# A hybrid attention and RWKV-7 encoder layer: gate products bound to the scan's products, two PSUM banks for the solved values, and PSUM tiles of its own for the first stage

## The chip, the cores and the metric

The kernel runs on one core of a Trainium2 chip, as one launch. The metric is the device time of that launch in microseconds (us); lower is better. TensorE (PE) multiplies, VectorE (DVE), ScalarE (ACT) and GpSimd (POOL) do the elementwise work, and SyncE (SP) issues the transfers between DRAM and the on-chip memory. Products land in PSUM, which has eight banks of 512 float32 columns.

## The reference

One layer over 1040 positions (16 learned ones and 1024 of the input) with 1024 channels. A normalised input is projected to everything that the two mixing branches need; the branches are merged through sigmoid gates; a gated MLP follows.

```python
proj = hn @ w_in
q, k, v, f_logit, rw, gates = jnp.split(proj, IN_SPLITS, axis=-1)
...
o_fox = fox_attention(qh, kh, vh, fcum)
...
def rwkv7_scan(r, w, k, v, a, bb):
    '''S_t = S_{t-1} diag(w_t) + (S_{t-1} a_t) bb_t^T + v_t k_t^T ;  y_t = S_t r_t.'''
...
yn = (y - mean) * lax.rsqrt(var + GN_EPS)
...
g_fox, g_rwkv = jnp.split(jax.nn.sigmoid(gates + g_b), 2, axis=-1)
merged = g_fox * (o_fox @ w_bf) + g_rwkv * (o_rwkv @ w_br)
```

The scan is the serial part: the state of one position enters the next. The gates depend on the normalised input alone.

## The kernel before

Channels lie on the 128 partitions and positions along the free dimension, in three chunks of some 340 to 386 columns. Float32 products are made as three products of rounded halves (`mm3`: high by high, low by high, high by low), so one tile of 1024 input channels takes 24 product instructions, three for each of eight slices of the channels. A scheduler orders each engine's instructions from the order in which the program emits them; each engine then works strictly in that order.

**Stage 0** (`stage0`) loads the input, takes root mean squares (`stats`, with `rsqrt_rows`, whose inverse root is a bit trick and Newton iterations on a few columns), writes the normalised input as high and low parts (`norm`), and makes three low-rank projections for each chunk (`lora`): twelve products a chunk (line 173), each copied out by ACT into a tile `o` (three buffers) and stored to DRAM by SP. Its products use the PSUM pool that later serves attention (tags `S` and `M`), and the low-rank products share the banks `A` and `B` (use `pr`) with the next stage.

**Stages 1 and 2** are three streams that are emitted side by side: `att` (attention), `rec` (first `prep`, the projections and factors of the scan, use `pr`; then the scan), and `gat` (the gates). The scan is cut into 17 chunks of 64 positions. A chunk (`rw_chain`) is a chain: eight products from the state (line 523, the right sides), a copy by ACT (525), eight products with the inverted triangle (534, the solved values), copies by ACT and DVE (535, 536), eight products for the next state (541), an addition by DVE (544); beside it 16 products give the chunk's output (549, 551), which goes to DRAM. Each chunk's operands come by nine transfers (`rw_load`, lines 497 to 506), one chunk ahead. The inversion itself (`solve`) is done for six chunks at a time. After chunks 5, 10 and 16 `group_norm` normalises the finished positions, with two products (873, 878) for each of four channel tiles.

**The gates** are 16 tiles by three chunks of 24 products each, 1152 in all, each chunk copied out by ACT (856) and stored. They are emitted once the scan's pool exists, 13 tiles at first and the last three once the scan has been emitted. Where they stand between the scan's products was up to the scheduler.

Stage 3 multiplies the branches by their output weights, stage 4 is the output projection with the second norm, stage 5 the MLP.

Of the kernel before, what the change touches and what calls it, by code (L numbers as in the profile page):

```python
# [102 lines left out]
def stage0(S):  # L103
# [8 lines left out]
    with tc.tile_pool(name="s0", bufs=1) as p0:  # L112
# [47 lines left out]
        def lora(c):  # L160
            t0, t1 = G[c]
            n = t1 - t0
            sg, wa = T("sg", 1), T("wa", 1)
            rw_tile(S, 0, sg[:, :n], w0[0], c)
            nc.scalar.activation(out=sg[:, :n], in_=sg[:, :n], func=AF.Tanh, scale=0.5)
            nc.gpsimd.tensor_scalar(out=sg[:, :n], in0=sg[:, :n], scalar1=0.5, scalar2=0.5, op0=ALU.mult, op1=ALU.add)
            rw_tile(S, 1, wa[:, :n], w0[1], c)
            nc.scalar.activation(out=wa[0:64, :n], in_=wa[0:64, :n], func=AF.Tanh)
            for p in range(NP_):
                pc = slice(p * P, (p + 1) * P)  # L170
                for i, (l, r) in enumerate(((lup[0:64, pc], wa[0:64, :n]), (lup[64:128, pc], wa[64:128, :n]), (gup[:, pc], sg[:, :n]))):
                    ps = psum(S, "pr")
                    nc.tensor.matmul(ps[:, :n], lhsT=l, rhs=r, start=True, stop=True)
                    o = T("o", 3)
                    if i == 2:
                        nc.scalar.copy(out=o[:, :n], in_=ps[:, :n])
                    else:
                        S.tanh = nc.scalar.activation(out=o[:, :n], in_=ps[:, :n], func=AF.Tanh, scale=0.5, bias=(S.w0h, S.a0h)[i][:, p:p + 1])
                    if i == 0:
                        nc.gpsimd.tensor_scalar(out=o[:, :n], in0=o[:, :n], scalar1=0.5, scalar2=0.5, op0=ALU.mult, op1=ALU.add)  # L180
                    nc.sync.dma_start(out=(S.sw_d, S.tha_d, S.g_d)[i][p, :, t0:t1], in_=o[:, :n])
# [57 lines left out]
def psum(S, tag):  # L239

    slots = S.psb[tag]
    n = S.psn[tag] % len(slots)
    S.psn[tag] += 1
    t = slots[n]
    if n and slots[n - 1] == t:
        return S.half[tag][:, 512:1024]
    S.half[tag] = slot(S, t, tag)
    return S.half[tag][:, 0:512]
# [261 lines left out]
def rw_chain(S, c):  # L510
    nc, rp = S.nc, S.rp
    if c == 0:
        S.ld_c = rw_load(S, 0)
    uv, w1, am, ar, bkt = S.ld_c
    if c < NCH - 1:
        S.ld_c = rw_load(S, c + 1)
    z, zn = S.zb[c % 2], S.zb[(c + 1) % 2]
    at = S.at[c // 6][:, 4 * (c % 6):4 * (c % 6) + 4]
    H = [(h, h // 2, h % 2, slice(64 * (h % 2), 64 * (h % 2) + 64)) for h in range(8)]
    quads = lambda ps: ps[:, :256].rearrange("p (q v) -> p q v", v=64)  # L520
    pv = quads(psum(S, "ch"))
    for h, q, e, r in H:
        nc.tensor.matmul(pv[r, q, :], lhsT=w1[:, h, :], rhs=z[e][:, q, :], start=True, stop=True)  # L523
    pt = rp.tile([P, 4, 64], F32, name="pt", bufs=1)
    nc.scalar.copy(out=pt[:], in_=pv)
    zw = rp.tile([P, 4, 64], F32, name="zw", bufs=1)
    if c < NCH - 1:
        for e in range(2):
            r = slice(64 * e, 64 * e + 64)
            nc.gpsimd.tensor_tensor(out=zw[r], in0=z[e][r], in1=S.wc[r, c, :].unsqueeze(2).broadcast_to([64, 4, 64]), op=ALU.mult)  # L530
    yield 1.0
    pu = quads(psum(S, "ch"))
    for h, q, e, r in H:
        nc.tensor.matmul(pu[r, q, :], lhsT=at[r, q, :], rhs=pt[r, q, :], start=True, stop=True)  # L534
    nc.scalar.copy(out=uv[0][0:64], in_=pu[0:64])
    nc.vector.tensor_copy(out=uv[1][64:128], in_=pu[64:128])
    yield 1.0
    if c < NCH - 1:
        pz = quads(psum(S, "ch"))
        for h, q, e, r in H:  # L540
            nc.tensor.matmul(pz[r, q, :], lhsT=bkt[:, q, r], rhs=uv[e][:, q, :], start=True, stop=True)  # L541
        for e in range(2):
            r = slice(64 * e, 64 * e + 64)
            nc.vector.tensor_tensor(out=zn[e][r], in0=pz[r], in1=zw[r], op=ALU.add)
        yield 1.0
    py = quads(psum(S, "ch"))
    for q in range(4):
        for h, _, e, r in H[2 * q:2 * q + 2]:
            nc.tensor.matmul(py[r, q, :], lhsT=z[e][:, q, :], rhs=ar[e][:, q, :], start=True, stop=False)  # L549
        for h, _, e, r in H[2 * q:2 * q + 2]:  # L550
            nc.tensor.matmul(py[r, q, :], lhsT=uv[e][:, q, :], rhs=am[:, h, :], start=False, stop=True)  # L551
    yt = rp.tile([P, 4, 64], F32, name="yt", bufs=1)
    nc.scalar.copy(out=yt[:], in_=py)
    n = min(64, L - 64 * c)
    nc.sync.dma_start(out=S.y_d[:, :, 64 * c:64 * c + n].rearrange("q p t -> p q t"), in_=yt[:, :, :n])
    yield 1.0
# [56 lines left out]
def rsqrt_rows(S, pool, ps, sq, n, ind, w, eps):  # L613
# [14 lines left out]
    nc.vector.tensor_scalar(out=v, in0=ps[:m, o:o + W], scalar1=eps, scalar2=None, op0=ALU.add)  # L628

    nc.vector.tensor_scalar(out=y.bitcast(I32), in0=v.bitcast(I32), scalar1=-0.5, scalar2=1597463007.0, op0=ALU.mult, op1=ALU.add)  # L630
    for _ in range(4):
        nc.vector.tensor_tensor(out=t, in0=v, in1=y, op=ALU.mult)
        nc.vector.scalar_tensor_tensor(out=t, in0=t, scalar=-0.5, in1=y, op0=ALU.mult, op1=ALU.mult)
        nc.vector.scalar_tensor_tensor(out=y, in0=t, scalar=1.5, in1=y, op0=ALU.add, op1=ALU.mult)
# [209 lines left out]
            now = t  # L844


def gates(S, ms):

    nc = S.nc
    for m in ms:  # L850
        w = wload(S, S.A["w_gate"][m], KD)
        for t0, t1 in CW:
            ps = psum(S, "gate")
            mm3(S, ps[:, :342], w, xwin(S, t0 + 2, 342))
            sg = S.cp.tile([P, 342], F32, name="sg", bufs=2)
            nc.scalar.activation(out=sg[:], in_=ps[:, :342], func=AF.Identity, bias=S.par("gate_b", m))  # L856
            nc.sync.dma_start(out=S.sg_d[m, :, t0 - T0:t1 - T0], in_=sg[:])
            yield 3.8


def group_norm(S, c):
# [29 lines left out]
def stage12(S):  # L891

    nc, tc = S.nc, S.tc
    banks(S, mm="S S M M", st="t o", pr="A B", t="t", o="o")
    pq_cm = tc.tile_pool(name="ps1", bufs=1, space=PSUM)
    S.pq = pq_cm.__enter__()
    p1_cm = tc.tile_pool(name="p1", bufs=1, side="right")
    p1 = p1_cm.__enter__()
    S.smask = p1.tile([P, 384], BF16, name="smask")
    nc.gpsimd.memset(S.smask[:], 1.0)  # L900
    nc.gpsimd.memset(S.smask[:].rearrange("p (c t) -> p c t", t=64)[:, :, 0:1], 0.0)
    stage0(S)
    banks(S, mm="S M")
    S.op = S.rp = None
    S.scanned = False
    S.ev = 0

    def att():
# [16 lines left out]
    def rec():  # L925
# [29 lines left out]

        S.of_cm = tc.tile_pool(name="of", bufs=1, side="right")
        S.ofp = S.of_cm.__enter__()
        S.scanned = True
        yield from merge_streams([(0.0, 1.0, group_norm(S, 2)), (0.0, 1.0, fox_load(S))])

    def gat():
        while S.rp is None:
            yield 1.0
        yield from gates(S, range(13))

        while not S.scanned:
            yield 1.0
        yield from gates(S, range(13, 16))

    for _ in merge_streams([(0.0, 1.0, att()), (0.0, 1.2, rec()), (0.0, 1.0, gat())]):  # L970
        pass
# [353 lines left out]
```

## Time and profile before

| | |
|---|---|
| median of 3 runs | 1916.93 us (1916.77 to 1916.99) |
| the profiled execution, its own time | 1909.92 us |
| its span, first to last instruction | 1908.1 us |
| PE busy | 1809.4 us, 95% |
| DVE, ACT, POOL busy | 57%, 40%, 39% |
| first low-rank product of the first chunk to last of the third | 41.05 to 108.7 us |
| first product of the scan | 738.26 us |
| last product of the scan | some 966.5 us |

The span is cut into stretches, and in each PE's busy time is multiplied by the clock that was granted to it (as a share of full speed): what is missing from the stretch's length is the time in which PE did not work at full pace.

### The profile page before, as it was taken

To read this page: it belongs to the slowest core of one execution; us is meant where nothing else is said; L and a number is where in the kernel's file an instruction comes from. 1 tells how busy PE (TensorE), PEld (TensorE's weight loads), DVE (VectorE), ACT (ScalarE), POOL (GpSimd) and SP (SyncE) were. 2 spreads that over 40 slices of the span, in tenths; PEclk is the share of its full clock that TensorE was granted. 3 is DMA by queue.
4 is the path that set the end of the run, shared out by engine and by line. 5 is a ranking of instruction groups with operands and counts; after the bars stand their busy time and mean duration, and the time that the engine had idled before them with its cause. 6 is when DMAs were issued, how large, how long until landed. Compare 5 with 4: busy or idle time off the path is not lost.

```text
span 1908.1 us, 33665 instructions
## 1 busy us (share of the span) xinstructions
PE 1809.4 (95%) x12756; PEld 1629.3 (85%) x12756; DVE 1086.0 (57%) x2024; ACT 764.4 (40%) x1684; POOL 748.4 (39%) x817
## 2 busy tenths in 40 slices
PE   5899999899999899999978999999999999999999
PEld 4589779679788588989868998998998999989997
DVE  6224644655746766632445538668567575585655
ACT  5345534443635532233455324433332332333331
POOL 4134224222414322233323235347346365474464
PEclk9899999799999899999998999999999999999999
DMA  5221331241423364675663334111112111111113
GB/s 179 102 66 46 81 82 54 68 105 53 99 65 82 77 150 123 169 192 162 190 177 113 116 117 126 45 45 47 48 39 67 45 38 63 51 40 56 45 45 116
DMA packets 197577, 170.83 MB, mean 90 GB/s; under 512 B 93768, under 2 KB 154744, under 8 KB 197416
## 3 DMA queue, kind: packets, MB, share of 16 engines
q1 hardware_dynamic: 197160, 168.62, 30.9%
q8 instruction: 101, 1.65, 0.4%
q14 instruction: 60, 0.49, 0.1%
q0 software_dynamic: 256, 0.07, 0.0%
HBM read 122.57 MB, written 46.06 MB: 88 GB/s over the span
## 4 chain that ended last, share of the span: by engine, by line
PE 57%; DVE 2%; DMA 2%; ACT 1%; POOL 1%; issue 1%; SPq 1%; ACTq 0%; DVEq 0%; POOLq 0%
PE mm L218 11%; PE mm L219 11%; PE mm L220 11%; PE dn L220 4%; PE dn L218 4%; PE dn L219 4%; PE gate L218 3%; PE gate L219 3%; PE gate L220 3%; DMA y<-y_d 1%; PE ch L541 1%; PE ch L534 0%; PE ch L523 0%; PE ch L551 0%; PE ch L549 0%
## 5 line engine op out<-in xcount | busy, mean ns | idle before, releaser
L206 POOL TENSOR_TENSOR wl<-wf,wh 128x512 fp32r<-128x512 f32 (+1 forms) x228 | 295.9, 1301 | 532.7 <-ACT wh L205 520.1
L219 PE MATMUL mm<-x,wh 128*128 128x344 f32 (+1 forms) x1056 | 338.5, 321 | 0.0
L220 PE MATMUL mm<-x,wl 128*128 128x344 f32 (+1 forms) x1056 | 336.9, 320 | 0.9 <-POOL wl L206 0.9
L218 PE MATMUL mm<-x,wh 128*128 128x344 f32 (+1 forms) x1056 | 336.6, 320 | 0.0
L205 ACT CAST wh<-wf 128x512 fp32r<-128x512 f32 (+1 forms) x228 | 138.7, 610 | 175.7 <-PE mm L219 70.4
L220 PEld LDWEIGHTS mm<-x,wl 128*128 128x128 f32 x1056 | 198.9, 189 | 1.7 <-POOL wl L206 1.5
L219 PEld LDWEIGHTS mm<-x,wh 128*128 128x128 f32 x1056 | 199.2, 189 | 0.4
L218 PEld LDWEIGHTS mm<-x,wh 128*128 128x128 f32 x1056 | 199.0, 189 | 0.5
L1171 DVE TENSOR_TENSOR h<-h,dn 128x512 f32<-128x512 f32 x240 | 153.1, 683 | 34.9 <-PE dn L220 28.6
L218 PE MATMUL gate<-xh,wh 128*128 128x342 f32 x384 | 127.4, 332 | 4.6 <-ACT sg L856 2.3
L219 PE MATMUL gate<-xl,wh 128*128 128x342 f32 x384 | 127.2, 331 | 0.0
L220 PE MATMUL gate<-xh,wl 128*128 128x342 f32 x384 | 126.6, 330 | 0.0
L218 PE MATMUL mm<-xh,wh 128*128 128x348 f32 (+5 forms) x336 | 116.9, 348 | 4.1 <-DVE sg L269 1.9
L219 PE MATMUL mm<-xl,wh 128*128 128x348 f32 (+5 forms) x336 | 113.9, 339 | 1.8 <-POOL xl L158 1.2
L220 PE MATMUL mm<-xh,wl 128*128 128x348 f32 (+5 forms) x336 | 112.5, 335 | 0.0
L218 PE MATMUL dn<-gx,wh 128*128 128x512 f32 x280 | 110.3, 394 | 0.0
L219 PE MATMUL dn<-gx,wh 128*128 128x512 f32 x280 | 110.2, 393 | 0.0
L220 PE MATMUL dn<-gx,wl 128*128 128x512 f32 x280 | 109.8, 394 | 0.0
L1138 DVE SCALAR_TENSOR_TENSOR uv<-mm,par,uv 128x342 f32<-128x342 f32 (+1 forms) x66 | 37.7, 571 | 108.9 <-ACT uv L1137 108.9
L218 PE MATMUL pr<-xh,wh 128*128 128x386 f32 (+1 forms) x288 | 95.9, 333 | 1.4 <-ACT bt L469 1.4
L220 PE MATMUL pr<-xh,wl 128*128 128x386 f32 (+1 forms) x288 | 94.8, 329 | 0.0
L219 PE MATMUL pr<-xl,wh 128*128 128x386 f32 (+1 forms) x288 | 94.8, 329 | 0.0
(326 smaller groups left out, 4325.2 us busy)
## 6 DMA issues: line engine op xcount, KB each, us to landing
wf<-in_w_up_dram SPq DMA_DIRECT2D x88, 256.0 KB, 2.7
wf<-in_w_down_dram SPq DMA_DIRECT2D x40, 256.0 KB, 2.7
sg_d<-sg SPq DMA_DIRECT2D x48, 171.0 KB, 3.3
sg<-sg_d SPq DMA_DIRECT2D x48, 171.0 KB, 2.3
wf<-in_w_gate_dram SPq DMA_DIRECT2D x32, 256.0 KB, 4.7
wf<-in_w_out_dram SPq DMA_DIRECT2D x32, 256.0 KB, 2.8
wf<-in_w_rw_dram SPq DMA_DIRECT2D x28, 256.0 KB, 2.7
wf<-in_w_qkv_dram SPq DMA_DIRECT2D x24, 256.0 KB, 2.9
```

The source lines that it names most:

```text
L205: nc.scalar.copy(out=wh[:, :n], in_=wf[:, :n])
L206: nc.gpsimd.tensor_tensor(out=wl[:, :n], in0=wf[:, :n], in1=wh[:, :n], op=ALU.subtract)
L218: nc.tensor.matmul(ps, lhsT=wh, rhs=xh, start=first and k == 0, stop=False)
L219: nc.tensor.matmul(ps, lhsT=wh, rhs=xl, start=False, stop=False)
L220: nc.tensor.matmul(ps, lhsT=wl, rhs=xh, start=False, stop=last and k == n - 1)
L541: nc.tensor.matmul(pz[r, q, :], lhsT=bkt[:, q, r], rhs=uv[e][:, q, :], start=True, stop=True)
L1138: nc.vector.scalar_tensor_tensor(out=t[:, :n], in0=ps[:, 1:1 + n], scalar=cw(1), in1=t[:, :n], op0=ALU.mult, op1=ALU.add)
L1171: nc.vector.tensor_tensor(out=half(r, c), in0=half(r, c), in1=ps[:], op=ALU.add if sign > 0 else ALU.subtract)
```

## The change

- **Gates.** One slice of the channels (three products, an eighth of a tile's chunk) is now emitted at a time, and each is ordered behind the latest of the scan's product groups (`S.hop`: the last product of lines 523, 535 and 542 of the new kernel). An eighth counts 0.53 in the streams' pacing while the scan runs and 0.33 before; a scan chunk counts 4.8, so nine eighths go with a chunk. All 16 tiles are one run; the wait for the scan's end is gone.
- **Two banks.** The solved values of the even and of the odd heads go to a PSUM bank each, so ACT and DVE copy from different banks.
- **The first stage** has a PSUM pool of its own: four single banks, two for its projections (`mm`) and two for the low-rank products (`lr`). The banks `A` and `B` are left to `prep`. The pool of attention is opened when stage 0's is closed. `o` has five buffers instead of three.
- `rsqrt_rows` makes three Newton iterations instead of four.

```diff
-                    ps = psum(S, "pr")
+                    ps = psum(S, "lr")
                     nc.tensor.matmul(ps[:, :n], lhsT=l, rhs=r, start=True, stop=True)
-                    o = T("o", 3)
+                    o = T("o", 5)
...
-    pu = quads(psum(S, "ch"))
+
+    pu = [quads(psum(S, "ch")) for _ in range(2)]
     for h, q, e, r in H:
-        nc.tensor.matmul(pu[r, q, :], lhsT=at[r, q, :], rhs=pt[r, q, :], start=True, stop=True)
-    nc.scalar.copy(out=uv[0][0:64], in_=pu[0:64])
-    nc.vector.tensor_copy(out=uv[1][64:128], in_=pu[64:128])
+        S.hop = nc.tensor.matmul(pu[e][r, q, :], lhsT=at[r, q, :], rhs=pt[r, q, :], start=True, stop=True)
+    nc.scalar.copy(out=uv[0][0:64], in_=pu[0][0:64])
+    nc.vector.tensor_copy(out=uv[1][64:128], in_=pu[1][64:128])
...
-    for _ in range(4):
+    for _ in range(3):
...
-def gates(S, ms):
+def gates(S):
...
-    for m in ms:
+    for m in range(16):
         w = wload(S, S.A["w_gate"][m], KD)
         for t0, t1 in CW:
             ps = psum(S, "gate")
-            mm3(S, ps[:, :342], w, xwin(S, t0 + 2, 342))
+            x = xwin(S, t0 + 2, 342)
+            for k in range(KD):
+                with S.tc.issue_after(S.hop.ins) if S.hop is not None else nullcontext():
+                    mm3(S, ps[:, :342], w[k:k + 1], x[k:k + 1], first=k == 0, last=k == KD - 1)
+                yield 0.53 if S.hop is not None else 0.33
...
-    banks(S, mm="S S M M", st="t o", pr="A B", t="t", o="o")
-    pq_cm = tc.tile_pool(name="ps1", bufs=1, space=PSUM)
-    S.pq = pq_cm.__enter__()
+
+    banks(S, mm="0 1", st="t o", lr="2 3", pr="A B")
...
-    stage0(S)
-    banks(S, mm="S M")
+    with tc.tile_pool(name="ps0", bufs=1, space=PSUM) as S.pq:
+        stage0(S)
+    pq_cm = tc.tile_pool(name="ps1", bufs=1, space=PSUM)
+    S.pq = pq_cm.__enter__()
+    banks(S, mm="S M", t="t", o="o")
```

How the instructions stand, at three places. First PE's queue in stage 0, at the low-rank products (line 173; `wa` and `sg` are their right sides, `lup` and `gup` the weights) of the second chunk. Before, they follow one another:

```order
L173 MATMUL pr<-wa,lup 128x384
L173 MATMUL pr<-sg,gup 128x384
L173 MATMUL pr<-wa,lup 128x384 x2
L173 MATMUL pr<-sg,gup 128x384
L173 MATMUL pr<-wa,lup 128x384 x2
L173 MATMUL pr<-sg,gup 128x384
L173 MATMUL pr<-wa,lup 128x384 x2
L173 MATMUL pr<-sg,gup 128x384
```

And now, at the same products:

```order
L173 MATMUL lr<-wa,lup 128x384
L219 MATMUL pr<-xl,wh 128x274
L220 MATMUL pr<-xh,wl 128x274
L173 MATMUL lr<-sg,gup 128x384
L218 MATMUL pr<-xh,wh 128x274
L219 MATMUL pr<-xl,wh 128x274
L220 MATMUL pr<-xh,wl 128x274
...
L173 MATMUL lr<-wa,lup 128x384 x2
L218 MATMUL pr<-xh,wh 128x386
L219 MATMUL pr<-xl,wh 128x386
L173 MATMUL lr<-sg,gup 128x384
```

The scan's input projections (`pr`) have moved in between. In all 96 of them (72 of 386 columns, 24 of 274) now stand ahead of stage 0's last low-rank product, where none did; 32 products of the forget gate's logits (line 580 of before), which stood ahead of it, now stand behind it. At the third group of attention's transposes (line 689 of before) both queues have the same products behind them.

Second, PE's queue in the scan's first chunk, between the right sides (523) and the solved values (534 before, 535 now); `wh` and `wl` are a gate tile's weights. Before, 22 gate products stand there, of which these are the last:

```order
L220 MATMUL gate_8080<-xh_97,wl_7830 128x342
L218 MATMUL gate_8080<-xh_98,wh_7829 128x342
L219 MATMUL gate_8080<-xl_106,wh_7829 128x342
L220 MATMUL gate_8080<-xh_98,wl_7830 128x342
L218 MATMUL gate_8080<-xh_99,wh_7829 128x342
L219 MATMUL gate_8080<-xl_107,wh_7829 128x342
L220 MATMUL gate_8080<-xh_99,wl_7830 128x342
L534 MATMUL ch_7998<-pt_7952,at_7028 64x64 x8
```

And now, all that stands there:

```order
L218 MATMUL gate_8037<-xh_94,wh_7823 128x342
L219 MATMUL gate_8037<-xl_102,wh_7823 128x342
L220 MATMUL gate_8037<-xh_94,wl_7824 128x342
L218 MATMUL gate_8037<-xh_95,wh_7823 128x342
L219 MATMUL gate_8037<-xl_103,wh_7823 128x342
L220 MATMUL gate_8037<-xh_95,wl_7824 128x342
L535 MATMUL ch_8103<-pt_8078,at_7026 64x64 x4
```

A chunk held 57 to 59 gate products before (22, 22, 1 to 3, and 12), until they ran out at its fifteenth chunk; now it holds 27 (6, 6 to 9, 6 to 9, 6). Ahead of the scan's first product stand 263 gate products before and 339 now.

Third, PE's queue behind the scan's last output product. Before, the gates are used up, and the branch products of stage 3 (`orw`, `ofx`) stand between the last statistics products (`gn`):

```order
L220 MATMUL mm<-orw,wl 128x342
L873 MATMUL gn<-y,bo_197 128x342
L218 MATMUL mm<-ofx,wh 128x342
L219 MATMUL mm<-ofx,wh 128x342
L220 MATMUL mm<-ofx,wl 128x342
```

And now:

```order
L219 MATMUL gate<-xl,wh 128x342
L220 MATMUL gate<-xh,wl 128x342
L218 MATMUL gate<-xh,wh 128x342
L878 MATMUL gn<-y,bo_197 128x342
L219 MATMUL gate<-xl,wh 128x342
L220 MATMUL gate<-xh,wl 128x342
```

From the scan's last solved values to the last statistics product 264 gate products now stand, 200 of them behind the first of the eight statistics products; the branch products come behind all of them, but for two.

## Rows read from the trace of the kernel before

**Rows 1.** Stretches: length, busy time (count) by engine, granted clock, DMA share, GB/s.

```profile
20.00:120.00 100.00, 83.61 (x347) 59.49 (x347) 36.46 (x82) 45.87 (x101) 29.64 (x46) 0.86 0.30 101
120.00:738.20 618.20, 579.09 (x4468) 498.51 (x4466) 362.16 (x809) 284.08 (x724) 190.83 (x230) 0.96 0.31 78
738.20:955.40 217.20, 212.79 (x2452) 191.19 (x2453) 90.32 (x195) 74.90 (x156) 67.42 (x74) 1.00 0.64 178
955.40:1020.00 64.60, 48.80 (x345) 39.69 (x342) 27.75 (x61) 39.70 (x73) 11.96 (x14) 0.84 0.49 143
1050.00:1100.00 50.00, 50.00 (x321) 50.00 (x320) 25.88 (x48) 18.50 (x39) 14.17 (x10) 1.00 0.38 116
```

**Rows 2.** PE in stage 0: start, length, instruction, [idle before, releaser].

```profile
19.40 0.66 PE L218 MATMUL mm<-xh,wh 128*128 128x386 f32 x1 [1.49 <-ACT xh L156]
...
28.91 0.34 PE L220 MATMUL mm<-xh,wl 128*128 128x386 f32 x1
...
60.11 0.34 PE L218 MATMUL mm<-xh,wh 128*128 128x386 f32 x1
...
64.16 0.34 PE L220 MATMUL mm<-xh,wl 128*128 128x386 f32 x1
...
75.84 1.65 PE L173 MATMUL pr<-sg,gup 128*128 128x384 f32 x2 [2.40 <-ACT o L178]
...
107.41 1.27 PE L173 MATMUL pr<-sg,gup 128*128 128x272 f32 x2 [0.39 <-ACT o L178]
```

**Rows 3.** Order of time, ACT in stage 0.

```profile
75.20 0.58 ACT L178 ACTIVATE o<-pr,lin_w 128x384 f32<-128x384 f32 x1 [2.73 <-DMA tha_d<-o]
...
107.89 1.28 ACT L191 ACT_TABLE_LOAD   x1
```

**Rows 4.** Order of time, PE in the scan.

```profile
738.26 0.69 PE L523 MATMUL ch<-zb,w 128*64 128x64 f32 x16
...
764.13 0.69 PE L523 MATMUL ch<-zb,w 128*64 128x64 f32 x16
...
957.53 0.68 PE L534 MATMUL ch<-pt,at 64*64 64x64 f32 x16 [0.52 <-ACT pt L525]
958.68 1.08 PE L541 MATMUL ch<-uv,bkt 128*64 128x64 f32 x15 [0.47 <-ACT uv L535]
```

**Rows 5.** The tile `ch`, the two copies: ns shortest/median/longest, first and last start.

```profile
L535 ACT COPY uv<-ch x17: 350/367/369, 743.3 to 963.4; 64x256 f32<-64x256 f32 x17
L536 DVE COPY uv<-ch x17: 427/428/428, 744.0 to 963.8; 64x256 f32<-64x256 f32 x17
```

**Rows 6.** Order of time, SP's queue in the scan, the loads of one chunk.

```profile
763.77 0.54 SPq L497 DMA_DIRECT2D zb<-v_d  x1
...
768.81 0.53 SPq L499 DMA_DIRECT2D w<-w_d  x1
```

**Rows 7.** Transfers, 738 to 960 us: packets, MB, share; issues, KB, us to landing.

```profile
q1 hardware_dynamic: 52509, 39.13, 63.7%
...
bkt<-bkt_d SPq DMA_DIRECT2D x15, 256.0 KB, 3.0
am<-am_d SPq DMA_DIRECT2D x14, 256.0 KB, 4.2
```

**Rows 8.** Order of time, PE behind the scan: the first and the last statistics products.

```profile
971.28 0.84 PE L873 MATMUL gn<-y,bo 128*128 128x342 f32 x2 [1.21 <-DMA y<-y_d]
...
1012.15 1.34 PE L878 MATMUL gn<-sq,bo 128*128 128x342 f32 x2
```

**Rows 9.** Order of time, DVE: two instructions of one Newton iteration in stage 0.

```profile
37.15 0.16 DVE L632 TENSOR_TENSOR rt<-rv,ry 128x3 f32<-128x3 f32 x1
...
37.54 0.16 DVE L634 SCALAR_TENSOR_TENSOR ry<-rt,ry 128x3 f32<-128x3 f32 x1
```

**Rows 10.** Stretches with small gaps: the columns of rows 1.

```profile
500.00:540.00 40.00, 36.64 (x373) 26.55 (x371) 34.00 (x91) 22.12 (x67) 6.12 (x12) 1.00 0.40 96
960.00:970.00 10.00, 7.26 (x101) 6.24 (x96) 1.20 (x3) 1.48 (x4) 0.00 (x0) 0.83 0.41 105
```

More of the change, by code (lines that the diff above doesn't have):

```diff
@@ L522, in rw_chain @@
     for h, q, e, r in H:
-        nc.tensor.matmul(pv[r, q, :], lhsT=w1[:, h, :], rhs=z[e][:, q, :], start=True, stop=True)
+        S.hop = nc.tensor.matmul(pv[r, q, :], lhsT=w1[:, h, :], rhs=z[e][:, q, :], start=True, stop=True)
     pt = rp.tile([P, 4, 64], F32, name="pt", bufs=1)
@@ L540, in rw_chain @@
         for h, q, e, r in H:
-            nc.tensor.matmul(pz[r, q, :], lhsT=bkt[:, q, r], rhs=uv[e][:, q, :], start=True, stop=True)
+            S.hop = nc.tensor.matmul(pz[r, q, :], lhsT=bkt[:, q, r], rhs=uv[e][:, q, :], start=True, stop=True)
         for e in range(2):
@@ L857, in gates @@
             nc.sync.dma_start(out=S.sg_d[m, :, t0 - T0:t1 - T0], in_=sg[:])
-            yield 3.8
 def group_norm(S, c):
@@ L901, in stage12 @@
     nc.gpsimd.memset(S.smask[:].rearrange("p (c t) -> p c t", t=64)[:, :, 0:1], 0.0)
-    stage0(S)
-    banks(S, mm="S M")
+    with tc.tile_pool(name="ps0", bufs=1, space=PSUM) as S.pq:
[3 more added lines that the diff above has]
+    banks(S, mm="S M", t="t", o="o")
     S.op = S.rp = None
-    S.scanned = False
+    S.hop = None
     S.ev = 0
@@ L957, in rec @@
         S.ofp = S.of_cm.__enter__()
-        S.scanned = True
         yield from merge_streams([(0.0, 1.0, group_norm(S, 2)), (0.0, 1.0, fox_load(S))])
@@ L963, in gat @@
             yield 1.0
[L964 to L968, printed above, removed]
+        yield from gates(S)
     for _ in merge_streams([(0.0, 1.0, att()), (0.0, 1.2, rec()), (0.0, 1.0, gat())]):
```

## The prediction, written before the changed kernel had run

> **What bounds the kernel now.** Read the stretches first [rows 1]. From 1050 us on PE is busy the whole time at the full level of its clock, 2.4 GHz: 321 products in 50 us, 0.156 us each, as at the steady pace of all 342-column products. Nothing of the change stands there but one Newton iteration, so the last 860 us are as good as fixed. What can be won lies ahead of it, where PE works below pace. Multiply busy time by granted clock and take it from the length: from 20 to 120 us 100 - 83.61 x 0.86 = 28.1 us are lost, from 120 to 738 us 618.2 - 579.09 x 0.96 = 62.3 us, in the scan 217.2 - 212.79 = 4.4 us, and behind it, from 955 to 1020 us, 64.6 - 48.80 x 0.84 = 23.6 us. PE's queue decides the end: time is gained by giving it ready products in those stretches and lost by making it wait elsewhere. The change touches the first, the third and the fourth.
>
> The queue in order of time tells why the first is thin [rows 2]: behind the normalised input only low-rank products are left to do, and a group of them waits 2.40 us for ACT, which itself waited 2.73 us for a store, since all three tiles `o` were under way [rows 3]. Behind the scan the gates are used up, and PE has eight statistics products with long elementwise chains between them: from 971.28 to 1013.49 us [rows 8].
>
> **Stage 0.** Now 96 projections stand between the low-rank products. One of 386 columns takes (64.16 - 60.11) / 23 = 0.176 us at full clock [rows 2], 72 of them 12.7 us; 24 of 274 columns, by the same rate, 3.0 us. That is 15.7 us of work in the holes. Against it 32 products of the forget gate now come behind, 32 x 0.156 = 5.0 us. So if the last low-rank product still came at 107.4 us, the gain would be 10.7 us: the lower bound. The upper bound is the whole 28 us. I take the value nearer the upper one, because the loras no longer share banks with anyone and have five tiles `o`: the holes themselves close. What stays lost I estimate at 7 us. First, the input's slices arrive one by one and the clock stands at its lower level at the start: 24 products took from 19.40 to 28.91 us, 0.32 us apart for a good part of it, and now 48 stand there, some 3 us over their pace. Second, the third chunk's norm comes behind more products than before, and PE has only 16 products and two loras while DVE writes it: 2 us. Third, attention's PSUM opens only behind the last copy of stage 0, and ACT has a table load of 1.28 us ahead of that copy [rows 3]: 2 us. So **21 us** (10.7 to 28).
>
> At the third group of transposes both queues have the same products behind them, and they run on alike up to the gates, so I let the 62 us of the middle stretch stand: everything there comes earlier, and nothing faster.
>
> **The scan.** Two steps before, from 738.26 to 764.13 us, hold 59 + 57 gate products [rows 4]: (25.87 - 116 x 0.156) / 2 = 3.9 us is the scan's own work in a step, changes of tile included. Now a step holds 27 gates: 3.9 + 27 x 0.156 = 8.1 us of PE work, against 12.9. The work is not less. The 76 gates that now stand ahead of the scan and the 264 behind it are taken out of it. What matters is whether each hop is still covered. Uncovered, at the end of the scan, PE waited 0.52 us for the copy of the right sides and 0.47 us for the first solved values [rows 4]. Six gates are 0.94 us: covered. For the solved values the second copy counts too, 0.37 us on ACT and then 0.43 us on DVE, one after the other in one bank [rows 5]; with two banks they may run together. Six to nine gates (0.94 to 1.40 us) cover either, so the two banks are worth nothing here; without cover they would be worth at most 17 x 0.43 = 7 us. The next state is covered by six to nine gates, 16 output products and six more gates.
>
> The loads are closer. A chunk's nine transfers are issued in a row from the moment the chunk before the last lets go of its tiles: from the first to the last 768.81 - 763.77 = 5.0 us, since a store and other transfers stand between them [rows 6]. A 256 KB transfer lands 3.0 to 4.2 us after its issue [rows 7]. So the last operand is there 8.0 to 9.2 us after the output products, and the product that wants it stands a step and six gates behind these, 8.1 + 1.0 = 9.1 us. SP's queue is only just fast enough. The bytes fit: some 1.3 MB of loads and store, 0.2 MB of gate results and 0.2 MB of gate weights in 8.1 us are 210 GB/s, and before 178 GB/s took 64% [rows 1, 7]; but statistics loads come in between twice. I take 0.35 us for 17 steps, **6 us lost** on top of the 4.4 (none to 24, if the queue holds every step to 9.5 us).
>
> **Behind the scan.** 264 gates are 41.2 us of ready work. 200 of them, 31.2 us, and eight statistics products of some 0.8 us lie in the 42.2 us that the chain took from the first statistics product to the last [rows 8], so 42.2 - 31.2 - 6.4 = 4.6 us stay open. The start, before the first statistics are loaded, is covered by 64 gates. Adding 3 us for a clock that dips in these holes, 8 of the 23.6 us stay: **16 us gained** (5 to 22).
>
> **The iterations.** Of the three dependent instructions that go, each start is 0.2 us behind the last (37.15 to 37.54 us is two such steps [rows 9]): 0.6 us where PE waits for a norm, in two of six calls. 1 us gained; bound below nothing, above 4.
>
> **The sum.** 21 - 6 + 16 + 1 = 32 us. The profiled execution took 1909.92 us, so 1878. The median of the runs shown is 0.37% above that execution; with the same difference the time is **1885 us**.
>
> **Rivals.**
> - *The holes of stage 0 close less* (chance 0.17). If the low-rank chain still paces stage 0, only the lower bound is gained, 10.7 us: 1895 us. For it: two PSUM banks as before, and a chain product, ACT, POOL, store. Against it: the waits seen were for tiles `o` and for left sides that nothing else covered.
> - *The loads pace the scan* (0.13). At 10 us a step instead of 8.5, 17 x 1.5 = 26 us are lost: 1885 + 26 = 1911 us at the worst, and some 1903 if half the steps are so. For it: SP's order, one queue, 5.0 us of issue. Against it: the 9.1 us above.
> - *The clock falls in the scan* (0.07), the one that ends slower. In 960 to 970 us, with the scan's chain alone on PE and 2.7 us idle, the granted clock was 0.83, so part of it stood at 1.2 GHz; from 500 to 540 us, with 8% idle in many small gaps, it stayed 1.00 [rows 10]. The new scan is short of cover only in small gaps, so I hold with the second. It decides from here: 17 steps hold 138 us of work; at a mean clock of 0.81 they take 32 us more, and the gain is gone; at 0.75 the time is 1885 + 46 = 1931 us. The Trainium skill (TensorE: Matmul & The Clock Gate, A second HAM failure mode: psum-queue depth-cycling) tells of a kernel whose products cycled through PSUM banks with short idle times between groups, and whose clock swung between its two levels although most products ran at the full one. By that rule the new scan, which goes round two banks five times a step, is at risk and the time would be the 1931 us; the trace of before agrees in its last steps and not in its middle stretch.
> - *It does better* (0.10): no hole in stage 0, and none behind the scan: 28 + 23.6 - 2 = 50 us, 1867 us.
> - *Given back* (0.03): the middle stretch loses what stage 0 gains, because attention and `prep` meet at other phases: within 0.2% of before.
>
> The forecast as above, 1873 to 1895 us, has 0.50. So faster by over 0.2%, which is about what a measurement of this kernel can tell from no change, 0.88; within it 0.05; slower 0.07. The range that leaves out the slower case, the last part of the loads' case and the end of the better one is 1864 to 1907 us; the likeliest's own is 1873 to 1895.
>
> **What would show it.** Right: the last low-rank product near 90 to 95 us, with projections between the loras and no wait for `o` above 1 us; the third group of transposes some 21 us before its place now; the scan's first products some 8.1 to 8.7 us apart a step, with waits under 0.5 us, and none for the solved values; statistics and gates in turn behind the scan, with a granted clock above 0.9; the same 50 us rows from stage 3 on. Wrong: PE waiting for `w`, `zb` or `arb` in most steps (the loads), a granted clock under 0.9 in the scan, or the last low-rank product behind 100 us. A sum that fits by errors that cancel would show in the stretches: each term has its own.

## The result and the profile after

The changed kernel takes 1885.54 us (median of 4, 1882.01 to 1892.9) against 1916.85 us for the kernel before (median of 4, 1904.99 to 1916.99). The ratio is 0.9857, with a 95% interval from 0.9809 to 0.9904: faster by 18 to 37 us. The forecast was 1885 us. Two executions further on stand far outside all others and are left out of the ratios: one of experiment 4 (3108.32 us) and one of the kernel before beside experiments 9 to 12 (4665.39 us).

The profiled execution is the longest of the four: 1892.9 us with a span of 1891.1 us, against 1909.92 and 1908.1 us before. So the two traces are only 17 us apart, and what they show has to be split into what the change did and what belongs to this execution. The stretches of the trace after, with the columns of [rows 1]; after the first row they end at the third group of attention's transposes, at the first product of the scan, at the first product of its last chunk, and behind the last statistics product:

```profile
20.00:120.00 100.00, 96.09 (x473) 73.97 (x472) 43.49 (x87) 51.29 (x113) 35.48 (x51) 0.91 0.34 110
125.59:738.72 613.13, 575.58 (x4376) 490.56 (x4373) 363.17 (x813) 277.21 (x708) 183.97 (x222) 0.94 0.31 79
738.72:924.73 186.01, 174.81 (x2213) 148.55 (x2208) 83.06 (x177) 61.54 (x135) 59.12 (x66) 0.94 0.70 184
924.73:1000.00 75.27, 70.70 (x478) 67.42 (x478) 28.68 (x53) 46.16 (x85) 24.27 (x22) 1.00 0.53 154
```

The kernel before, cut at the same places of the program:

```profile
144.86:738.26 593.40, 554.29 (x4312) 473.73 (x4310) 352.16 (x793) 275.11 (x704) 181.63 (x220) 0.95 0.31 79
738.26:960.90 222.64, 216.89 (x2554) 194.72 (x2554) 92.34 (x199) 76.43 (x159) 69.77 (x76) 1.00 0.64 178
960.90:1030.00 69.10, 54.63 (x296) 45.89 (x297) 30.24 (x65) 41.70 (x76) 15.58 (x16) 0.85 0.44 130
```

The first row of after answers to the first of [rows 1]: 83.61 us busy have become 96.09. In a long stretch the clock's two digits leave 3 us open, so for the table each stretch was read in slices of 5 us: idle time of PE, and the half of its busy time at 1.2 GHz, both in us. The second figure is an upper one: the stretch up to the scan took 13.8 us less in the profile of experiment 6 than here (599.3 against 613.1 us) with 19.9 us less of it and nearly the same idle time.

| stretch, idle + at the lower clock | before | after | stage 0 alone | without stage 0 |
|---|---|---|---|---|
| start to third transposes | 31.4 + 11.0 | 17.2 + 7.5 | 18.1 + 5.7 | 29.5 + 16.1 |
| to the scan | 39.1 + 21.5 | 37.5 + 32.6 | 37.8 + 14.4 | 35.9 + 9.5 |
| scan, up to its last chunk | 5.7 + 0 | 11.2 + 9.1 | 4.0 + 0 | 14.2 + 9.5 |
| behind it | 14.5 + 8.1 | 4.6 + 0 | 14.7 + 11.3 | 4.4 + 2.7 |

(The last two columns are experiments 2 and 3, below.) The third transposes in the kernel before:

```profile
144.86 0.49 PE L689 MATMUL t<-ident,v 128*128 128x128 f32 x3
```

PE of the changed kernel in order of time:

```profile
17.40 0.98 PE L218 MATMUL mm<-xh,wh 128*128 128x386 f32 x2 [1.34 <-POOL wl L206]
...
94.73 1.28 PE L173 MATMUL lr<-sg,gup 128*128 128x272 f32 x2
97.84 0.51 PE L581 MATMUL mm<-xh,wfh 128*40 128x348 f32 x1 [1.83 <-ACT o L176]
...
125.59 0.49 PE L690 MATMUL t<-ident,v 128*128 128x128 f32 x3
...
738.72 0.69 PE L523 MATMUL ch<-zb,w 128*64 128x64 f32 x16
...
744.66 0.48 PE L550 MATMUL ch<-arb,zb 128*64 128x64 f32 x4 [1.76 <-DVE uv L537]
...
759.81 0.69 PE L523 MATMUL ch<-zb,w 128*64 128x64 f32 x16
...
767.75 0.69 PE L523 MATMUL ch<-zb,w 128*64 128x64 f32 x16
```

The last low-rank product stands at 94.73 us instead of 107.41 [rows 2], the third transposes at 125.59 instead of 144.86. The scan begins at the same time as before [rows 4], but with 76 more gates, 11.9 us of work, already done. A step without anything between its hops but its 27 gates takes 7.94 us. Five of the 16 steps up to the last chunk are such undisturbed ones; the others hold an inverse's products, statistics products or 81 gates as well, or waits, and take up to 24.7 us. Two of the rows carry waits of nearly 2 us; all of PE's waits in the scan together:

```profile
PE gn L878 <- DMA y<-y_d: 5.0, 3, 2.2
PE sv L330 <- DVE hs L321: 2.2, 2, 1.9
PE ch L550 <- DVE uv L537: 1.8, 1, 1.8
PE ch L542 <- ACT uv L536: 0.9, 2, 0.5
PE ch L535 <- ACT pt L525: 0.6, 1, 0.6
PE ch L542 <- DVE uv L537: 0.5, 1, 0.5
```

None is for a load of the chain's operands. They are for statistics inputs (5.0 us), for copies by DVE (4.5) and by ACT (1.5). The statistics inputs are nothing new: before, PE waited 3.3 us for them in the scan, and 1.0 us for copies by ACT.

```profile
PE gn L873 <- DMA y<-y_d: 3.3, 3, 1.8
```

The waits for copies by DVE are new. DVE's queue in order of time shows why two of them are late:

```profile
743.18 0.97 DVE L309 STREAM_TRANSPOSE hs<-at 32x768 f32<-32x768 f32 x1 [3.28 <-DMA at<-x_d]
744.18 0.43 DVE L537 COPY uv<-ch 64x256 f32<-64x256 f32 x1
...
780.30 0.21 DVE L297 TENSOR_TENSOR x<-x,xm 104x30 f32<-104x30 f32 x1
780.54 1.04 DVE L321 COPY hs<-sv 32x384 f32<-32x384 f32 x2
```

The second copy of the solved values stands behind a transposition that waits for a load. The copies of one inverse's products (`hs`) stand behind the last elementwise pieces of the next inverse (lines 295 and 297, the last of them at 780.30 us). Something else has changed there as well: no gate stands between the inverse's groups of products any more, since every gate is bound to a hop of the chain. After, and then before, where 16 gates stand between the first two of these rows and 20 more ahead of the third, and PE waits for no copy:

```profile
777.58 1.71 PE L317 MATMUL sv<-hs,at 32*32 32x32 f32 x96
781.16 2.40 PE L330 MATMUL sv<-at,hs 32*32 32x32 f32 x96 [1.88 <-DVE hs L321]
```

```profile
792.79 0.95 PE L317 MATMUL sv<-hs,at 32*32 32x32 f32 x48
...
796.39 0.85 PE L317 MATMUL sv<-hs,at 32*32 32x32 f32 x42
...
801.29 0.95 PE L330 MATMUL sv<-at,hs 32*32 32x32 f32 x48
```

(The profile counts two records for each float32 product of the chain and of the inverse.) How busy DVE is does not explain the waits by itself: in three undisturbed steps it was busy for 21.86 of 23.98 us, and PE waited for nothing. In the whole scan its share went only from 41% to 45% (92.34 of 222.64 us and 83.06 of 186.01).

```profile
751.84:775.82 23.98, 23.98 (x322) 20.61 (x321) 21.86 (x50) 6.11 (x14) 6.10 (x7) 1.00 0.73 196
```

The lower clock in the scan, from stretches of the trace after:

```profile
744.00:751.00 7.00, 6.34 (x59) 5.74 (x60) 4.03 (x9) 1.44 (x3) 2.68 (x4) 0.51 0.73 189
782.00:788.00 6.00, 6.00 (x83) 5.33 (x78) 1.45 (x3) 1.48 (x3) 0.00 (x0) 0.50 0.45 144
857.00:863.00 6.00, 5.54 (x60) 4.69 (x58) 1.26 (x3) 0.83 (x2) 0.00 (x0) 0.50 0.59 158
```

These are the three places in the scan where the clock was low. The first two follow the waits of 1.76 and 1.88 us; the third begins among an inverse's products of 32 columns (160 records), with no gate between them. But the longest wait of the scan, 2.23 us, was followed by no fall:

```profile
902.59 0.81 PE L878 MATMUL gn<-y,bo 128*128 128x342 f32 x2 [2.23 <-DMA y<-y_d]
```

```profile
900.00:908.00 8.00, 5.76 (x66) 4.14 (x65) 3.11 (x8) 2.32 (x5) 2.46 (x3) 1.00 0.78 208
```

So what makes the clock fall here is not shown.

### The profile page after: what moved, and what is told of

It is laid out like the page before. It is cut to its first block, busy times and chain, and to the rows that moved or that the text cites. A ratio compares the mean times of both kernels' runs of the same rounds, so it can differ in the third digit from the quotient of the medians.

```text
span 1891.1 us, 33652 instructions
## 1 busy us (share of the span) xinstructions
PE 1813.6 (96%) x12756; PEld 1632.2 (86%) x12756; DVE 1091.7 (58%) x2006; ACT 761.1 (40%) x1684; POOL 752.4 (40%) x817
## 3 DMA queue, kind: packets, MB, share of 16 engines
q1 hardware_dynamic: 197160, 168.62, 31.4%
## 4 chain that ended last, share of the span: by engine, by line
PE 77%; DVE 8%; ACT 3%; DMA 3%; issue 2%; POOL 1%; SPq 1%; DVEq 0%; POOLq 0%; ACTq 0%
PE mm L219 13%; PE mm L218 13%; PE mm L220 13%; PE dn L220 4%; PE dn L218 4%; PE dn L219 4%; PE pr L218 2%; PE pr L219 2%; PE pr L220 2%; PE gate L218 2%; PE t L809 2%; PE o L822 2%; PE pr L442 2%; PE gate L219 2%; PE gate L220 1%
## 5 line engine op out<-in xcount | busy, mean ns | idle before, releaser
L218 PE MATMUL gate<-xh,wh 128*128 128x342 f32 x384 | 134.2, 349 | 2.2 <-ACT sg L862 2.2
```

What stands on the lines that cost most here:

```text
L218: nc.tensor.matmul(ps, lhsT=wh, rhs=xh, start=first and k == 0, stop=False)
```

## The experiments

Each group of four kernels was timed on one chip, beside the kernel before: that took 1911.86 us (median) beside experiments 1 to 4, 1909.28 beside 5 to 8 and 1912.44 beside 9 to 12. The ratios are against these. Run 1 is the run of experiment 1, and so on.

**1. The changed kernel again.** No edit.

> The changed kernel as it is, a second time, for the spread of its executions and a second profile. Its first profile stands at 1892.9 us, the other three executions at 1882.0 to 1885.7, and PE's clock was low in nine pieces of that profile, 113 us in all, four of them of 17 to 20 us. Theory A: what differs between executions is the length and the place of these low pieces, each piece of 20.5 us at 1.2 GHz costing 10 us; then a second profile has its third transposes again at 125 to 126 us, its undisturbed scan steps again at 7.9 to 8.1 us, and differs from the first only where the clock is low, with a span of 1880 to 1891 us. Theory B: the waits themselves differ; then steps and waits of the scan differ by more than 0.5 us while the clock stands alike.

Measured: 1884.85 us (1881.08 to 1892.29), ratio 0.9857 (0.9833 to 0.9881). The second profile is nearly a copy of the first, the lower clock's places included; the scan in it:

```profile
738.81:924.06 185.25, 175.49 (x2213) 148.77 (x2208) 82.89 (x177) 61.60 (x135) 58.97 (x66) 0.94 0.70 184
```

It is once more the longest execution. Spans and mean granted clocks of the six go roughly together: 1890.5 us at 0.970, 1886.9 at 0.975, 1884.8 at 0.972, 1881.3 at 0.978, 1881.1 at 0.979, 1879.3 at 0.980. Theory A is supported as far as these means go; where the clock stood in the unprofiled five is not shown. One of PE's waits does differ between the two profiles while the clock stands alike, as B has it: the statistics inputs cost 2.9 us in the scan here, against 5.0 in the first profile.

```profile
PE gn L878 <- DMA y<-y_d: 2.9, 4, 1.0
```

So the profile of after stands some 7 us above its median. That of before stood 7 us below the median of the runs shown with it, and 2 us below the median of the 17 executions timed here.

**2. Stage 0's part alone.** On the kernel before:

```diff
-                    ps = psum(S, "pr")
+                    ps = psum(S, "lr")
...
-                    o = T("o", 3)
+                    o = T("o", 5)
...
+    banks(S, mm="0 1", st="t o", lr="2 3", pr="A B")
...
+    with tc.tile_pool(name="ps0", bufs=1, space=PSUM) as S.pq:
+        stage0(S)
...
```

> The kernel before with only the first stage's part of the change: its own set of banks for the low-rank products and the projections, and five tiles for the products' results. Gates, solved values and Newton as before. Theory A (the stage's own banks and tiles close its holes, 17 to 19 us, and the stretch up to the scan gives some 8 of them back): the third group of transposes at 126 to 128 us instead of 144.9, and 1898 to 1908 us. Theory B (the stage's gain is all given back, and the whole gain of the change comes from the gates): third transposes early, but the time at 1913 to 1918. Theory C (nothing is given back, the 8 us belong to the gates ahead of the scan): 1896 to 1899 us.

Measured: 1889.5 us, 22.4 us less than before (17.0 to 26.6), ratio 0.9886 (0.9861 to 0.9911). The third transposes, and the stretches behind them:

```profile
126.14 0.49 PE L689 MATMUL t<-ident,v 128*128 128x128 f32 x3
```

```profile
126.14:714.84 588.70, 550.92 (x4300) 468.02 (x4298) 350.60 (x792) 274.13 (x703) 182.01 (x220) 0.97 0.31 80
714.84:935.00 220.16, 216.12 (x2542) 194.17 (x2543) 91.61 (x198) 76.43 (x159) 69.91 (x76) 1.00 0.66 180
935.00:1010.00 75.00, 60.36 (x337) 51.60 (x333) 35.61 (x72) 43.29 (x80) 17.13 (x16) 0.82 0.43 123
```

A and B fall: nothing is given back. The idle time up to the scan is that of before (37.8 against 39.1 us), and scan and tail are those of before. C is nearest, though the time is 6.5 us under its band.

**3. The change without stage 0's part.** The edit of 2 taken back in the changed kernel.

> The changed kernel with the first stage as it was before: gates bound to the scan in eighths, two banks and three Newton iterations stay. Theory A (binding gives 19 us behind the scan and costs 16 in the scan; with the iterations some 4 us remain): 1905 to 1915 us, third transposes back at 143 to 145 us. Theory B (the change's gain is that of the gates): 1885 to 1892 us. Prediction's own terms (16 - 6 + 1 = 11 us without the first stage): 1904 to 1907 us.

Measured: 1904.63 us, ratio 0.9958 (0.9939 to 0.9976), 7.2 us less than before. Scan and tail:

```profile
744.30:933.75 189.45, 175.31 (x2212) 148.66 (x2207) 82.69 (x177) 61.53 (x135) 59.32 (x66) 0.94 0.69 180
933.75:1010.00 76.25, 71.83 (x471) 68.83 (x471) 27.34 (x51) 45.31 (x82) 23.54 (x21) 0.96 0.54 155
```

They are nearly those of the changed kernel: the scan's loss and the tail's gain belong to this part of the change, and as runs 5 and 6 find no effect of the banks and the iterations on the time, to the gates. B falls. The time is that of the prediction's own terms, but the kernel before took 5 us less beside this experiment than in the runs from which they were worked out; by the difference, 7.2 us, it lies between A's 4 and the prediction's 11. 22.4 + 7.2 = 29.6 us, and both parts together gave 27.0 on the same chip: they add up within what the medians can tell.

**4. Gates in eighths, not bound.**

```diff
-                with S.tc.issue_after(S.hop.ins) if S.hop is not None else nullcontext():
+                with nullcontext():
```

> The changed kernel without the binding: an eighth of a gate step may stand anywhere its operands allow, nothing else differs. By the order on PE some 56 gate products then stand in a step, none is left behind the 14th step, and gates stand between the products of the inverse's blocks. Theory A (the binding is worth what the stretch behind the scan wins, 19 us, less what the scan loses, 16): scan steps of 12.7 to 13 us without waits, 20 to 25 us lost again behind the scan, and 1885 to 1893 us in all, within 8 us of the changed kernel. Theory B (the covered tail is a clear gain): 1897 to 1905 us.

Measured: 1900.45 us, ratio 0.9931 (0.9909 to 0.9953), 15.6 us more than bound. From the 14th step on:

```profile
928.77:1010.00 81.23, 56.73 (x483) 46.54 (x483) 36.91 (x78) 45.66 (x87) 18.19 (x20) 0.83 0.55 155
```

81.23 - 56.73 x 0.83 = 34.1 us are lost behind the last gate. B holds: the gates kept for the end are a clear gain. Against the whole tiles of the kernel before the binding's gain is smaller, 4.7 us on the new first stage (run 2 less run 1, the banks and iterations included, and within the noise of the two) and 7.2 on the old one (run 3), since there the gates lasted two steps longer.

**5. One bank for the solved values.**

```diff
-    pu = [quads(psum(S, "ch")) for _ in range(2)]
+    pu = [quads(psum(S, "ch"))] * 2
```

> The changed kernel with one bank for the solved values, as before, so that the two copies of a step (0.37 us on ACT, 0.43 us on DVE) stand one after the other. Theory A (the prediction's: six to nine gate products cover either way): undisturbed steps again at 7.9 to 8.1 us, no new wait in most steps, 1882 to 1888 us. Theory B (the second bank is what lets a step be this short): a wait of some 0.4 us in most of the 17 steps, steps of 8.4 us, 1889 to 1893 us.

Measured: 1883.85 us, ratio 0.9858 (0.9834 to 0.9882): no difference from the changed kernel. The first step has one long wait, and not for the bank:

```profile
740.37 1.11 PE L542 MATMUL ch<-uv,bkt 128*64 128x64 f32 x14 [4.59 <-DVE uv L537]
```

```profile
738.03 1.97 DVE L309 STREAM_TRANSPOSE hs<-at 32x768 f32<-32x768 f32 x2 [4.91 <-DMA at<-x_d]
```

It is the same transposition, two in a row. The shortest steps stay at 7.95 us, and only four waits in the scan are for DVE's copy of the solved values. A holds: the second bank is worth nothing that the time can show. PE was idle for 15.5 us of the scan in this profile, against 9.8 to 11.8 us in those of runs 1, 6 and 9, most of the difference in this one wait.

**6. Four Newton iterations.** `range(3)` back to `range(4)`.

> The changed kernel with four Newton iterations again. Theory A (the prediction's 1 us, each iteration 0.6 us where PE waits for a norm): the first group of low-rank input products 0.5 to 1.3 us later than 17.4 us in the changed kernel, third transposes at 126 to 127 us, 1885 to 1888 us. Theory B (a norm later by 0.6 us shifts what meets what, at the first stage or behind the scan): over 1890 us.

Measured: 1884.83 us, ratio 0.9858 (0.9836 to 0.988). The first input product stands 1.33 us later than in the changed kernel, third transposes at 128.6 us:

```profile
18.73 0.98 PE L218 MATMUL mm<-xh,wh 128*128 128x386 f32 x2 [1.55 <-ACT xh L156]
```

PE's wait for the inverse root grows from 2.54 to 3.12 us, 0.58 us, as predicted for one call; most of the rest is a first statistics product that stands 0.54 us later, which the trace does not explain. A is nearest, though its bands are missed: the transposes come 1.6 us behind its 127 us, and the time is 0.2 us under its 1885. In the time the iteration can't be seen.

**7. Both copies of the solved values on ACT.**

```diff
-    nc.vector.tensor_copy(out=uv[1][64:128], in_=pu[1][64:128])
+    nc.scalar.copy(out=uv[1][64:128], in_=pu[1][64:128])
```

> The changed kernel with both copies of the solved values on ACT, so that none stands in DVE's queue behind the next blocks' elementwise work. Theory A (in the shorter steps DVE's queue is late: in the first step the second copy stands behind a transposition that waits for a load): the wait of 1.8 us in the first step goes, and with it the piece at the lower clock behind it, scan 3 to 6 us shorter, 1879 to 1884 us. Theory B (two copies on ACT, 0.74 us one after the other, are no faster than ACT and DVE side by side): waits of 0.3 to 0.5 us for ACT's copy in many steps, 1885 to 1892 us.

Measured: 1882.33 us, ratio 0.9849 (0.9827 to 0.9871); scan, up to its last chunk, 181.26 us instead of 186.01 (and of 185.25, 184.10 and 183.05 in the profiles of runs 1, 6 and 9, whose copies stand as in the changed kernel). The first step takes 8.95 us without the long wait, as A has it. But PE now waits before the next chunk's first products, 2.7 us in two places; PE, then DVE, at the longer of them:

```profile
765.48 0.69 PE L523 MATMUL ch<-zb,w 128*64 128x64 f32 x16 [1.62 <-issue]
```

```profile
764.14 0.33 DVE L295 TENSOR_TENSOR xm<-x 104x168 f32<-104x168 f32 x1
764.50 0.88 DVE L545 TENSOR_TENSOR zb<-ch,zw 64x256 f32<-64x256 f32 x2
```

The products start 0.1 us behind the state's addition on DVE, which stands behind the elementwise pieces; DVE is busy for 16.44 of the 17.59 us from 747.89 on. The trace names no releaser, so that the addition is what they wait for is read from the times.

**8. A third tile for each of the statistics' loads.**

```diff
-        y, bon, g = T("y", 2), T("bon", 2), T("g", 2)
+        y, bon, g = T("y", 3), T("bon", 3), T("g", 3)
```

> The changed kernel with three tiles instead of two for each of the statistics' three loads, in the scan and behind it. Theory A (the waits for these loads, 5.0 us in the scan's steps and 3.2 us behind them in the first profile of the changed kernel, come from loads that wait in SP's queue for a tile to be let go): these waits fall below 3 us in all, and 1879 to 1884 us. Theory B (the loads are late for another reason, the store of the chunk just scanned or other loads ahead of them in the queue): the waits stay at 6 to 8 us, and the time at 1883 to 1888 us.

Measured: 1883.24 us, ratio 0.9859 (0.9835 to 0.9883). PE's waits in the scan:

```profile
PE gn L878 <- DMA y<-y_d: 2.4, 3, 1.5
```

The waits for these loads are 2.4 us in the scan, and none is left behind it. That is under A's 3 us, but it does not show that the third tile did it: with two tiles they were 5.0 us in the first profile of the changed kernel, 2.9 in the second, and 2.8 in that of run 6, which had none behind the scan either. Behind the scan another wait has grown, from 1.3 to 5.3 us:

```profile
PE gn L883 <- ACT sq L881: 5.3, 2, 3.3
```

The time lies in both bands and doesn't separate A from B.

**9. Three tiles `o` instead of five** in the changed kernel.

> The changed kernel with three tiles for the low-rank products' results instead of five; the first stage's own banks stay. Theory A (the tiles close the holes: before, PE waited 2.40 us for ACT and ACT 2.73 us for a store of a tile): the last low-rank product at 100 to 104 us instead of 94.7, third transposes at 130 to 135 us instead of 125.6, 1890 to 1896 us. Theory B (the projections that stand between the low-rank products on PE cover the waits whatever the tiles do): third transposes at 125 to 128 us, 1882 to 1887 us.

Measured: 1887.98 us, ratio 0.987 (0.9844 to 0.9895). The stage ends where it does with five, as B has it; the time is 1 us above B's band, 2 us under A's, and its ratio's interval overlaps that of run 1:

```profile
125.50 0.49 PE L690 MATMUL t<-ident,v 128*128 128x128 f32 x3
```

**10. 18 gates a chunk instead of 27.** `yield 0.53` becomes `yield 0.80`.

> The changed kernel with a pause of 0.80 instead of 0.53 behind each eighth: 18 gate products a chunk instead of 27, so 3.9 + 18 x 0.156 = 6.7 us of PE work in a step. Theory A (PE's own work sets the step, the loads have room): undisturbed steps of 6.6 to 7.0 us, waits only for copies, of 0.3 to 0.8 us. Theory B (the prediction's rival, the loads pace the scan at 8.0 to 9.2 us): steps stay at 8 us or more with PE waiting for the loads' tiles of the state, the writes or the reads. Either way some 150 more gates stand behind the scan than the statistics products there can use, so no gain: 1883 to 1892 us by A, 1890 to 1900 by B.

Measured: 1893.24 us, ratio 0.9901 (0.987 to 0.9932), some 8 us more than 27 a chunk, by the ratios. The start of the last step, and of the last chunk:

```profile
880.89 0.69 PE L523 MATMUL ch<-zb,w 128*64 128x64 f32 x16
...
887.76 0.69 PE L523 MATMUL ch<-zb,w 128*64 128x64 f32 x16
```

6.87 us: the loads keep up with a step that is 1.1 us shorter, so B falls on the steps, though the time lies in its band and 1 us above A's. 161.39 us of scan hold 148.19 busy ones: 13.2 us of waiting, 2 us more than with 27. Where the rest of the 8 us goes is not shown; this profile is of one of the two shortest of the six executions.

**11. Edits 7 and 8 together**, and **12. these, with the inverse's copies on ACT and the chain's pause in halves**:

```diff
-            (nc.vector.tensor_copy if e else nc.scalar.copy)(out=hs[z:z + 32, f:f + m], in_=pv[z:z + 32, :m])
+            nc.scalar.copy(out=hs[z:z + 32, f:f + m], in_=pv[z:z + 32, :m])
...
-                    yield t
                     for _ in range(2):
+                        yield t / 2
                         next(nxt, None)
```

> The changed kernel with both copies of the solved values on ACT and three tiles for each of the statistics' loads, the two edits that shortened the scan one by one. Theory A (they remove different waits and add up): idle time in the scan at 4 to 6 us instead of 11.2, 1877 to 1881 us. Theory B (each only moves PE to the next wait): idle time at 8 us or more, 1881 to 1885 us.

> The kernel of the run before it with the copies of the inverse's blocks on ACT as well, and the chain's pause split in two, so that a piece of the next inverse stands behind each half and a few gate products stand between its two groups of 48. Theory A (these copies come late because they stand in DVE's queue behind the next blocks' elementwise work, 1.6 to 2.7 us in the step with the inverse's first products): that wait falls under 0.5 us, 1875 to 1880 us. Theory B (the copies wait for their products' end as long on ACT): the wait stays over 1 us and the time is that of the run before it.

Measured: 1884.99 us, ratio 0.9855 (0.9831 to 0.988), and 1882.95 us, ratio 0.984 (0.9814 to 0.9866). In 12 the scan up to its last chunk is the shortest at 27 gates a chunk, 177.80 us, with 7.9 us idle. Among its waits there:

```profile
PE sv L330 <- ACT hs L321: 1.0, 2, 0.6
```

The wait for the inverse's copies is 1.0 us against 1.5 in 11, and another 1.0 us before the same products has no releaser named, so moving them helps less than A has it, though only two gates stand between the first of those groups here, and the wait before the next chunk's first products stays at 2.9 us. B is nearer for 12, and holds for 11 (8.9 us idle). No version is faster than the changed kernel by more than the measurement can tell.

## Why the prediction was right, point by point

**The total** is right, and so are the signs of the three large terms; the fourth, the iterations, is too small to be seen. One term, the scan's, was mis-sized, and its reason was wrong.

**Stage 0: 21 us predicted, 22.4 measured alone (17.0 to 26.6).** In the trace of after the third transposes come 19.3 us earlier. The holes did close: PE's waits from 40 to 110 us fell from 12.1 to 3.4 us. Of the reasons given, the five tiles `o` do nothing measurable (run 9), so that step is refuted; what is left is the low-rank products' own banks and the projections that stand between them, which no run takes apart. 100 - 96.09 x 0.91 = 12.6 us stay lost from 20 to 120 us, not 7: PE's clock was at 1.2 GHz from about 85 to 102 us, behind the projections, where only low-rank products were left. The 2 us for opening attention's PSUM were there, as the wait of 1.83 us for the last copy.

**The middle: no change predicted.** Idle time agrees (39.1 and 37.5 us); the lower clock took 11 us more in this execution. In the profiles of runs 2, 3 and 6 it took 14.4, 9.5 and 12.7 us, run 6 being the changed kernel but for the iterations, and the gain of stage 0 arrived in full, so the change does not give it back here. Why the clock falls for longer in some executions stays open.

**The scan: 6 us lost predicted, 14.6 in the trace (20.3 against 5.7).** This is the step that failed, even if the lower clock, counted in full here, costs somewhat less. By the same reading the profiles of runs 6 and 9, whose executions stand 0.8 and 2.1 us under their medians, lose 17.6 and 16.4 us, so that the miss does not come from this execution alone. The undisturbed steps are as worked out, 7.94 to 8.07 us for a predicted 8.1 of PE work, and the loads pace nothing, down to 6.87 us (run 10): the 6 us put down to SP's queue are not there. In their place PE waited 4.5 us for copies by DVE, where it waited for none before, and the lower clock, put at nothing for the scan, took 9.1 us (4.5 to 9.1 in the four profiles), where it took none before; the statistics inputs add 1.7 us in this profile and nothing in the second (5.0 and 2.9 against 3.3 before). The idle time alone grew by 5.5 us, near the 6 by chance. Two things were overlooked: what stands ahead of the second copy of the solved values in DVE's queue (waits were expected "under 0.5 us, and none for the solved values"), and that gates bound to the chain's hops no longer cover the inverse's products. How much of the 2.2 us waited for the inverse's copies belongs to the missing gates and how much to DVE's queue is not shown; run 12 moved the copies, but put only two or three gates there. And the sum counted 17 steps as 138 us of work: the 16 up to the last chunk took 186.01 us, of which 20.3 were lost, since the inverses, the statistics and the two steps with 81 gates were left out. With the bank taken away (run 5) the time is the same, so the two banks' price of nothing was right.

**Behind the scan: 16 us predicted, 18.0 in the trace** (22.6 less 4.6), the clock at 1.00. **Newton: 1 us predicted**; 0.58 us at one norm is shown, the whole is below what the times can tell.

Together the gates, banks and iterations were to bring 11 us and brought 7.2 (4.6 to 11.7): the time alone does not refute the 11; the trace speaks against it. The profiled execution was to take 1878 us and took 1892.9: here the scan's 8.6 us and the middle's clock are missing. That the median still fits rests on a second estimate, the profile's place among the executions: it was taken from before, 0.37% below the median, and came out above it. And beside run 1 the kernel before took 1911.86 us, so that the gain is 27.0 us and not 32: the terms promise 5 us too much, and the 1916.93 us from which the forecast started stand 5 us above that median. So the nearness of the total is partly luck; the two terms, measured apart, miss by 1.4 and 3.8 us.

**The rivals.** The holes of stage 0 closed. The loads don't pace. The clock did fall in the scan, three times, to a mean of 0.94, well above the 0.81 from which it would have decided. In the undisturbed steps the groups took turns on two banks with PE busy for 23.98 of 23.98 us, and the clock stood at 1.00. The section that the prediction named (the Trainium skill, TensorE: Matmul & The Clock Gate, A second HAM failure mode: psum-queue depth-cycling) tells of idle times between the groups; these steps had none, so they are no test of it. Where PE did wait, the clock fell behind waits of 1.76 and 1.88 us and not behind 2.23, so the trace neither bears that section out nor refutes it; the 1931 us that the rival gave did not come.

## What to carry to other kernels

Work that depends on nothing is best kept for the places where a chain leaves the engine empty. Held back for the tail it was worth 15.6 us against the same pieces unheld, and 4.7 to 7.2 us against the whole tiles of the kernel before, while the scan's hops needed only six to nine products each. When filler work is bound to one chain, look for what else it used to cover: the products of the inverse stood bare and PE waited there. And see what stands ahead of each copy in its engine's queue; a transposition that waits for a load held up a copy that was ready. Before a gain is read from two profiles, see where each stands among its kernel's executions.

## What the runs showed of the hardware

The executions of one kernel differed by 11 us (the changed one in run 1) and by 17 us (the one before beside it), and in run 1 the spans go roughly with the mean granted clock (1890.5 us at 0.970, 1879.3 at 0.980). Two profiles of the same kernel showed the lower clock at the same places, with 32.6 and 32.7 us counted for it in the stretch up to the scan; the profile of run 6, with one more iteration, showed 12.7 us there. In the scan the clock fell to 1.2 GHz behind waits of 1.76 and 1.88 us, and also among the 32-column products of an inverse behind a wait of only 0.35 us, but stayed at 2.4 GHz behind one of 2.23 us. In undisturbed steps, with 342-column products between groups of 64 columns, it stayed at 1.00.
